# Two more weight buffers, x^T at two addresses and a longer entry into the feed-forward, in a two-layer retention and attention trunk

## The chip, the cores and the metric

The kernel runs on one core of a Trainium2 chip. The metric is the device time of one execution in microseconds (us).

## The reference

512 tokens of width 1024 pass through two layers. Layer 0 mixes tokens by retention, layer 1 by dilated attention; each mixer and each feed-forward is added to 1.41 x and normalised.

```python
def swiglu_ffn(x, w_up, w_down):
    gate, up = jnp.split(x @ w_up, 2, axis=-1)      # D_FF = 2816 each
    return (jax.nn.silu(gate) * up) @ w_down

for i in range(DEPTH):                              # DEPTH = 2
    mix = retention(x, ...) if i % 2 == 0 else dilated_attention(x, ...)
    x = _layer_norm(DEEPNORM_ALPHA * x + mix, ln_gain[i, 0], ln_bias[i, 0])
    x = _layer_norm(DEEPNORM_ALPHA * x + swiglu_ffn(x, w_up[i], w_down[i]), ...)
```

## The kernel before

**Products.** Every large operand is split into a high and a low float32r part, and each product is three matmuls (`mm3`): high by high, high by low, low by high. The activations are kept transposed (`xhi`, `xlo`, called x^T here) and in rows (`r0` to `r3`, four blocks of 128 tokens).

**Weights.** `Weights` streams blocks of 128x1024 f32 (512 KB) in the order of a plan that is written down ahead. A load (SP queue, L77) takes one of six buffers `wraw`; load n needs the buffer of load n-6 to have been used up. ACT copies a block to `whi` (L133) and DVE subtracts to get `wlo` (L134); four pairs of them exist.

**Feed-forward.** The up-projection is done by Strassen-Winograd: the gate and the up half of 256 columns each form a *quad*, which takes seven *parts* instead of eight: B11, B21, T2, T1, T3, B22, T4. A part is 24 matmuls of 128x256 (8 positions times 3). The x side of a part is a combination of quarters of x^T made once (`x_sums`, `x_more`; the names of parts are the names of these tiles, B11, B21, B22 and T1 lie in x^T itself). The weight side is, for parts T2, T3 and B22, a sum of blocks that DVE makes for each quad (`make_sum`, L107: `sum2`, `sum4`, `sum5`). A quad loads four blocks, n to n+3. `sum2` is block n minus block n+2, into which block n+3 has been added by a second, accumulating transfer from HBM (`add_blocks`, issued by POOL, L89), which can only start once n+2 has landed. After a part, ACT copies the bank (`copied`, L739) since the next part goes on adding in it: T3 may only start when `u2`, the copy after T2, is made. DVE adds B11's copy and B21 (L752), and ACT takes the SiLU (L753).

There are 11 quads per feed-forward, in chunks of 4, 4 and 3, and after each chunk the down-projection `rows_product` adds to `r`. `make_sum` for a quad is called when the part before it is split, so the sums of the next quad stand in DVE's order among the work of this one. A scheduler then sets each engine's order.

**Entry.** The last `rows_product` of a mixer finishes one row block after the other: add (L454), layer norm (`ln`, L344 to L353), eight transposes (`flush`, then `to_xt`, L387), ACT's copies with gain and bias (L403), splits (L275, L276). The first chunk therefore begins with `up_pending`: B11 and B21 of two quads need only the early blocks; `up_late` then does quad 0 in the order B22, T1, T2, T4, T3. In attention's last `rows_product` the last pair's quotients (`att_norm`, L1120, L1121) come in four parts of 128 tokens.

**Addresses.** Worked out from the sizes of the pools, x^T, the T tiles, the feed-forward's h, retention's z, q, k, v and s all begin 32 bytes past a multiple of 128 in each partition; `whi` and `wlo` begin 96 past.

Of the kernel before, what the change touches and what calls it, by code (L numbers as in the profile page):

```python
# [37 lines left out]
S0 = 7 * P  # L38

# [109 lines left out]
def trunk(tc, a, out):  # L149
# [41 lines left out]
    with tc.tile_pool(name="const", bufs=1) as cpool, tc.tile_pool(  # L191
        name="xpool", bufs=1
    ) as xpool, tc.tile_pool(name="wraw", bufs=6) as wraw, tc.tile_pool(
        name="pad", bufs=1
    ) as pad, tc.tile_pool(name="whl", bufs=4) as whl, tc.tile_pool(name="lnp", bufs=2) as lnp, tc.tile_pool(
        name="ps", bufs=8, space=PSUM
    ) as ps, tc.tile_pool(name="scratch", bufs=1, space=DRAM) as dr:
        pad.tile([P, 80], F32, name="pad")
        ws = Weights(nc, plan, wraw, whl, 2, 6)
# [48 lines left out]
class Core:  # L248
    def __init__(self, nc, tc, a, out, ws, cpool, xpool, lnp, ps, dr):
        self.nc, self.tc, self.a, self.out, self.ws = nc, tc, a, out, ws  # L250
        self.lnp, self.ps, self.dr = lnp, ps, dr
        self.xhi = xpool.tile([P, KT, T], F32R, name="xhi")
        self.xlo = xpool.tile([P, KT, T], F32R, name="xlo")
# [7 lines left out]
        nc.gpsimd.dma_start(out=self.cols, in_=a["ln_cols"])  # L261
        self.on_read = False
        self.pending = []
        self.halves = False

# [66 lines left out]
    def next_halves(self, i):  # L332


        self.halves, self.of = True, i

# [119 lines left out]
    def rows_product(self, zs, first, last, final=False, have=(), without=(), finish=False):  # L456
# [15 lines left out]
        w = [*have] + [self.ws.get() for _ in range(n - early - len(have))]  # L472
        for b in range(NB):
            if not early:
                banks.update({(b, h): self.bank() for h in range(2)})
# [13 lines left out]
            if last:  # L489
# [4 lines left out]
                if b == 2 and not final:  # L494
# [7 lines left out]
    def retention(self):  # L502
        nc, tc, a = self.nc, self.tc, self.a
        with tc.tile_pool(name="rt", bufs=1) as rt:
# [6 lines left out]
            nc.sync.dma_start(out=self.sin, in_=a["sin"])  # L511
            qk = self.ret_qk()
# [4 lines left out]
            self.next_halves(0)  # L517
            for h in range(RH):
# [12 lines left out]
                else:  # L531
# [6 lines left out]
                    z = self.ret_z(g, tr)  # L538
                    self.rows_product(z, False, True)
# [156 lines left out]
    def ffn(self, i):  # L696
        nc, tc = self.nc, self.tc
        with tc.tile_pool(name=f"ff{i}", bufs=1) as ff:
# [7 lines left out]
            self.x_late = {}  # L706
            for n in ("T2", "T3", "T4"):
                self.xs[n] = [ff.tile([P, 4, T // 2], F32R, name=f"{n}{p}") for p in ("hi", "lo")]
            for ch, n in enumerate(FC):
# [10 lines left out]
                self.halves = False  # L720
                self.rows_product(zs, ch == 0, last, final=last and i == 1, finish=ch == 0)
# [99 lines left out]
    def attention(self, first, steps):  # L821
        nc, tc = self.nc, self.tc
        with tc.tile_pool(name="at", bufs=1) as at:
# [6 lines left out]
            self.half = at.tile([P, HD], F32, name="half")  # L830
            nc.vector.memset(self.half, 1.0)
# [16 lines left out]
    def bias_rows(self):  # L848
# [6 lines left out]
        nc.gpsimd.dma_start(out=rb[0:32, :], in_=self.a["rbT"])  # L855
        nc.gpsimd.dma_start(out=oh0, in_=self.a["onehot"][:, 0:W0])
        nc.gpsimd.dma_start(out=oh1, in_=self.a["onehot"][:, W0:WB])
# [223 lines left out]
    def att_pv(self, p, _):  # L1081
# [25 lines left out]
        for h in range(2):  # L1107
            self.mm(den[h * HD : (h + 1) * HD], self.half, e[:, h], True, True)
        self.pv = bk, den, e

    def att_norm(self, p, _):
# [6 lines left out]
        for c in range(parts):  # L1118
# [3 lines left out]
            self.split(hi[:, c], lo[:, c], zf[:, c])  # L1122
        self.zs[p] = (hi, lo)

# [123 lines left out]
```

## Time and profile before

| | us |
|---|---|
| median of 3 runs (1700.6 to 1705.23) | 1703.7 |
| the profiled execution | 1714.11 |
| its span, from first to last instruction | 1712.3 |
| TensorE busy in it | 1654.3 |
| VectorE (DVE) busy | 1067.7 |
| ScalarE (ACT) busy | 648.4 |
| GpSimd (POOL) busy | 220.5 |

PE is the matmul engine. Its mean granted clock is 0.982 of full speed. A line such as L270 is that of `mm`, through which all products go, so groups of matmuls are told apart by their tiles.

### The profile page before, as it was taken

What the parts mean: (1) busy time and instruction counts of PE and PEld (TensorE: products, weight loads), DVE (VectorE), ACT (ScalarE), POOL (GpSimd) and SP (SyncE); (2) the same over time, 40 slices, a digit from 0 to 9 for tenths busy, and PEclk for the clock granted to TensorE, in tenths of its full rate; (3) what the DMA queues carried; (4) which work ended last, traced back from release to release, by engine and by line L of the source; (5) the groups of instructions that cost most, each with busy time, mean ns of one, the idle gap of its engine ahead of it and who ended that gap; (6) DMA issues with size and microseconds to landing.
All of it is one profiled execution on the core that took longest, in us unless ns stands there. A gap on an engine that the chain in (4) does not pass through costs nothing. (4 is left out here: it accounts for less than half of the span.)

```text
span 1712.3 us, 24333 instructions
## 1 busy us (share of the span) xinstructions
PE 1654.3 (97%) x9972; PEld 1432.7 (84%) x9972; DVE 1067.7 (62%) x1391; ACT 648.4 (38%) x937; POOL 220.5 (13%) x307
## 2 busy tenths in 40 slices
PE   9999999999899899899999999999999899989997
PEld 6888888888898898899878788788877898888896
DVE  6454454647994674657265574567569995575565
ACT  4322232325652451444332332333233752443351
POOL 0000000000000000006232332233311000000002
PEclk9999999999999999899999999999999999999999
DMA  7322223222453433433232223223321444334321
GB/s 276 129 71 96 74 72 101 87 74 79 126 166 106 115 114 94 114 111 100 98 95 79 86 87 87 87 76 97 88 74 50 117 130 148 99 112 134 90 84 50
DMA packets 52896, 174.33 MB, mean 102 GB/s; under 512 B 7764, under 2 KB 9828, under 8 KB 52784
## 3 DMA queue, kind: packets, MB, share of 16 engines
q1 hardware_dynamic: 44272, 155.81, 27.1%
q0 software_dynamic: 8512, 16.97, 5.6%
q8 instruction: 78, 1.28, 0.3%
q14 instruction: 34, 0.28, 0.1%
HBM read 170.57 MB, written 2.17 MB: 101 GB/s over the span
## 5 line engine op out<-in xcount | busy, mean ns | idle before, releaser
L134 DVE TENSOR_TENSOR wlo<-wraw,whi 128x1024 fp32r<-128x1024 f32 (+1 forms) x278 | 339.8, 1228 | 361.2 <-ACT whi L133 360.1
L133 ACT ACTIVATE whi<-wraw 128x1024 fp32r<-128x1024 f32 (+1 forms) x278 | 292.7, 1055 | 675.3 <-PE bank L270 357.7
L270 PE MATMUL bank<-xhi,whi 128*128 128x256 f32 (+1 forms) x1376 | 459.4, 334 | 9.1 <-ACT xhi L275 8.4
L270 PE MATMUL bank<-xhi,wlo 128*128 128x256 f32 (+1 forms) x1376 | 456.3, 332 | 3.6 <-DVE wlo L134 3.6
L270 PE MATMUL bank<-xlo,whi 128*128 128x256 f32 (+1 forms) x1376 | 455.8, 331 | 1.5 <-DVE xlo L276 1.5
L270 PEld LDWEIGHTS bank<-xhi,whi 128*128 128x128 f32 x1376 | 261.3, 190 | 40.2 <-ACT xhi L275 11.4
L270 PEld LDWEIGHTS bank<-xhi,wlo 128*128 128x128 f32 x1376 | 261.4, 190 | 32.5 <-DVE wlo L134 4.8
L270 PEld LDWEIGHTS bank<-xlo,whi 128*128 128x128 f32 x1376 | 261.6, 190 | 28.3 <-DVE xlo L276 2.1
L270 PE MATMUL bank<-whi,hlo 128*128 128x512 f32 x352 | 138.7, 394 | 0.0
L270 PE MATMUL bank<-wlo,hhi 128*128 128x512 f32 x352 | 138.0, 392 | 0.0
L270 PE MATMUL bank<-whi,hhi 128*128 128x512 f32 x352 | 136.8, 389 | 0.0
L882 POOL DMA_DIRECT2D tab<-rows_dram x128 | 69.5, 552 | 198.5 <-DVE s L1006 196.1
L133 ACT ACTIVATE whi<-sum 128x1024 fp32r<-128x1024 f32 x66 | 70.1, 1063 | 62.6 <-PE bank L270 51.9
L89 POOL DMA_DIRECT2D wraw<-in_w_up_dram x22 | 19.1, 869 | 559.3 <-DMA wraw<-in_w_up_dram 276.0
L454 DVE TENSOR_TENSOR r<-r,bank 128x512 f32<-128x512 f32 x78 | 52.3, 683 | 57.3 <-PE bank L270 57.3
L270 PE MATMUL bank<-whi,xlo 128*128 128x512 f32 (+1 forms) x256 | 86.0, 336 | 0.0
L270 PE MATMUL bank<-whi,xhi 128*128 128x512 f32 (+1 forms) x256 | 86.0, 336 | 0.0
L270 PE MATMUL bank<-wlo,xhi 128*128 128x512 f32 (+1 forms) x256 | 85.7, 335 | 0.0
L134 DVE TENSOR_TENSOR wlo<-sum,whi 128x1024 fp32r<-128x1024 f32 x66 | 80.4, 1220 | 8.1 <-ACT whi L133 8.1
L270 PE MATMUL bank<-T3hi,whi 128*128 128x256 f32 x176 | 57.8, 328 | 25.6 <-ACT tmp L739 25.6
L270 PEld LDWEIGHTS bank<-wlo,hhi 128*128 128x128 f32 x352 | 66.1, 188 | 15.1
L270 PEld LDWEIGHTS bank<-whi,hhi 128*128 128x128 f32 x352 | 66.1, 188 | 14.4
(279 smaller groups left out, 3006.2 us busy)
## 6 DMA issues: line engine op xcount, KB each, us to landing
wraw<-in_w_up_dram SPq DMA_DIRECT2D x88, 512.0 KB, 3.6
wraw<-in_w_aqk_dram SPq DMA_DIRECT2D x48, 512.0 KB, 3.5
wraw<-in_w_dn_dram SPq DMA_DIRECT2D x44, 512.0 KB, 3.6
wraw<-in_w_av_dram SPq DMA_DIRECT2D x24, 512.0 KB, 3.5
wraw<-in_w_up_dram POOLq DMA_DIRECT2D x22, 512.0 KB, 6.5
wraw<-in_w_rv_dram SPq DMA_DIRECT2D x16, 512.0 KB, 4.2
wraw<-in_w_rg_dram SPq DMA_DIRECT2D x16, 512.0 KB, 4.9
wraw<-in_w_ro_dram SPq DMA_DIRECT2D x16, 512.0 KB, 3.5
```

Source lines behind the costliest of these rows:

```text
L89: self.nc.gpsimd.dma_start(out=self.raw_tiles[u], in_=a[n + 3], accum_op=ALU.add)
L133: self.nc.scalar.activation(hi[:, c], src[:, c], AF.Copy)
L134: self.nc.vector.tensor_tensor(out=lo[:, c], in0=src[:, c], in1=hi[:, c].bitcast(F32), op=ALU.subtract)
L270: self.nc.tensor.matmul(out=out, lhsT=lhsT, rhs=rhs, start=start, stop=stop, skip_group_check=self.on_read)
L454: nc.vector.tensor_tensor(out=dst, in0=dst, in1=bk, op=ALU.add)
L882: self.nc.gpsimd.dma_start(out=tab[r * RUN : (r + 1) * RUN, h, b * P : (b + 1) * P].rearrange("p (r l) -> p r l", r=RES), in_=src(h * WB + ...
```

## The change

It has these parts:

1. `wraw` has eight buffers. Room comes from the removed `half` tile and pad, and from halving `dynamic_dma_scratch_size` (16384 by default, now 8192). The pools stand in another order.
2. x^T lies in a tile that is 128 floats longer, at offset 0 for retention and attention, and at offset 48 floats (192 bytes) while a feed-forward reads it (`place_x`). The T tiles get a pad of the same size ahead. By the sizes of the pools, everything now begins 96 bytes past a multiple of 128, weights too, except x^T in the feed-forward and the T tiles, which begin 32 past as before.
3. `up_pending` takes three quads instead of two: q0 B11, transposes, q0 B21, q1 B11, transposes, and so on. `up_late` still does quad 0.
4. The last pair's quotients are not issued together but one block at a time, inside `rows_product`.
5. In attention's last `rows_product`, transposes are called for after products (1,1) and (3,0) of block 3, not at block 2 and after (1,0).
6. The loads of `cols`, the bias rows' operands (`rbT`, `onehot`) and the first two `decay` tables go from POOL's queue to SP's.

```diff
-                todo.sort(key=lambda t: (t[1] if t[0] < 2 and t[1] < 2 else 2))
-                todo[4:9] = [(0, j) for j in (5, 3, 2, 6, 4)]
+                todo.sort(key=lambda t: t[0] >= EARLY or t[1] > 1)
+                todo[2 * EARLY : 2 * EARLY + 5] = [(0, j) for j in (5, 3, 2, 6, 4)]
...
-        ws = Weights(nc, plan, wraw, whl, 2, 6)
+        ws = Weights(nc, plan, wraw, whl, 2, 8)
...
-        self.xhi = xpool.tile([P, KT, T], F32R, name="xhi")
-        self.xlo = xpool.tile([P, KT, T], F32R, name="xlo")
+        self.xt = [xpool.tile([P, KT * T + P], F32R, name=n) for n in ("xhi", "xlo")]
+        self.place_x(0)
...
+    def place_x(self, shift):
+        self.xhi, self.xlo = [
+            t[:, shift : shift + KT * T].rearrange("p (k t) -> p k t", t=T) for t in self.xt
+        ]
...
         w = [*have] + [self.ws.get() for _ in range(n - early - len(have))]
+        at = ((1, 1), (3, 0)) if have else ((1, 0),)
         for b in range(NB):
+            while self.norm_parts and self.norm_parts[0][0] <= b + 1:
+                self.norm_parts.pop(0)[1]()
...
-                if last and not final and b == 3 and (i, h) == (1, 0):
+                if last and not final and b == 3 and (i, h) in at:
                     self.flush(1)
...
-                if b == 2 and not final:
+                if b == 2 and not final and not have:
                     self.flush(1)
...
-        nc.gpsimd.dma_start(out=dec, in_=self.a["decay"][h])
+        (nc.sync if h < 2 else nc.gpsimd).dma_start(out=dec, in_=self.a["decay"][h])
...
+            ff.tile([P, SHIFT], F32, name="pad")
             for n in ("T2", "T3", "T4"):
...
-                    quads = [self.up_late(*first[0]), self.up_rest(*first[1])]
+                    quads = [self.up_late(*first[0])]
+                    quads += [self.up_rest(*t) for t in first[1:]]
...
-        a = [self.up_first() for _ in range(2)]
-        self.flush(1)
-        a[0] = self.up_second(a[0])
-        self.flush()
-        a[1] = self.up_second(a[1])
-        return a
+        res = []
+        for _ in range(EARLY):
+            t = self.up_first()
+            self.flush(1)
+            res.append(self.up_second(t))
+        return res
...
-        nc.gpsimd.dma_start(out=rb[0:32, :], in_=self.a["rbT"])
+        nc.sync.dma_start(out=rb[0:32, :], in_=self.a["rbT"])
...
-    nc = bacc.Bacc("TRN2", target_bir_lowering=False, num_devices=1)
+    nc = bacc.Bacc("TRN2", target_bir_lowering=False, num_devices=1, dynamic_dma_scratch_size=8192)
```

**First place: DVE in the first quad of the second chunk.** The names are numbered here: before, blocks n, n+1, n+2 and n+3 of the next quad are `wraw_4375`, `wraw_4381`, `wraw_4393` and `wraw_4573`; now they are `wraw_4313`, `wraw_4345`, `wraw_4377` and `wraw_4384`. Before:

```order
L134 TENSOR_TENSOR wlo_4504<-sum2_4391,whi_4503 128x1024
L134 TENSOR_TENSOR wlo_4535<-wraw_4310,whi_4534 128x1024
L134 TENSOR_TENSOR wlo_4568<-sum4_4538,whi_4567 128x1024
L107 TENSOR_TENSOR sum2_4706<-wraw_4375,wraw_4393 128x1024
L752 TENSOR_TENSOR tmp_4564<-tmp_4531,bank_4533 128x512
L134 TENSOR_TENSOR wlo_4605<-sum5_4571,whi_4604 128x1024
```

Now (L109 is the old L107, L136 the old L134, L769 the old L752):

```order
L136 TENSOR_TENSOR wlo_4506<-sum2_4394,whi_4505 128x1024
L136 TENSOR_TENSOR wlo_4537<-wraw_4248,whi_4536 128x1024
L109 TENSOR_TENSOR sum2_4709<-wraw_4313,wraw_4377 128x1024
L136 TENSOR_TENSOR wlo_4570<-sum4_4540,whi_4569 128x1024
L109 TENSOR_TENSOR sum4_4776<-sum2_4709,wraw_4384 128x1024
L769 TENSOR_TENSOR tmp_4566<-tmp_4533,bank_4535 128x512
L136 TENSOR_TENSOR wlo_4608<-sum5_4573,whi_4607 128x1024
```

The next quad's `sum2` stands one row earlier, and its `sum4` now stands ahead of the addition that the SiLU waits for. In the later quads of a chunk `sum2` stands ahead of L809 (the old L792) instead of behind it.

**Second place: DVE at the first feed-forward's entry,** from the layer norm of the last row block on; `sum2`, `sum5` and `sum4` are quad 0's. Before:

```order
L350 BN_AGGR mv_3193<-st_3189 128x2
L134 TENSOR_TENSOR wlo_3248<-wraw_2935,whi_3247 128x1024
L323 TENSOR_SCALAR veps_3196<-mv_3193 128x1
L107 TENSOR_TENSOR sum2_3251<-wraw_2746,wraw_2987 128x1024
L353 TENSOR_SCALAR r3_86<-r3_86,mv_3193,rs_3194 128x1024
L107 TENSOR_TENSOR sum5_3253<-sum2_3251,wraw_2882 128x1024
L276 TENSOR_TENSOR xlo_80<-hlo_3289,xhi_79 128x4x128
L428 TENSOR_TENSOR hhi_3305<-hlo_3289,xw0_81 128x512
L107 TENSOR_TENSOR sum4_3445<-sum2_3251,wraw_2993 128x1024
L276 TENSOR_TENSOR xlo_80<-hhi_3305,xhi_79 128x4x128
L430 TENSOR_TENSOR hhi_3305<-hhi_3305,hlo_3289 128x512
L134 TENSOR_TENSOR wlo_3314<-sum5_3253,whi_3313 128x1024
```

Now:

```order
L359 BN_AGGR mv_3193<-st_3189 128x2
L109 TENSOR_TENSOR sum2_3372<-wraw_2567,wraw_2987 128x1024
L331 TENSOR_SCALAR veps_3196<-mv_3193 128x1
L348 TENSOR_TENSOR r0_79<-r0_79,gain_3204 128x1024
L362 TENSOR_SCALAR r3_82<-r3_82,mv_3193,rs_3194 128x1024
L284 TENSOR_TENSOR xlo_76<-hlo_3253,xhi_75 128x4x128
L437 TENSOR_TENSOR hhi_3269<-hlo_3253,xw0_77 128x512
L136 TENSOR_TENSOR wlo_3278<-wraw_2779,whi_3277 128x1024
L439 TENSOR_TENSOR hhi_3269<-hhi_3269,hlo_3253 128x512
L284 TENSOR_TENSOR xlo_76<-hhi_3269,xhi_75 128x4x128
L769 TENSOR_TENSOR tmp_3305<-tmp_3246,bank_3276 128x512
L284 TENSOR_TENSOR T2lo_3211<-hhi_3269,T2hi_3210 128x4x128
```

Quad 0's `sum5` comes eight rows further down, after the splits of two more early parts. On PE one part (B21 of quad 1, 24 matmuls) stood between the last transposes and quad 0's B22; now three stand there (B21 of quad 1, B11 and B21 of quad 2, 72 matmuls).

**Third place: SP's queue at the start,** from the second head's gate weights on (`rv`, `rg`, `rqk` are retention's weights). Before:

```order
L77 DMA wraw<-in_w_rg_dram 128x1024 x4
L77 DMA wraw<-in_w_rqk_dram 128x1024
L516 DMA r_85<-in_x_dram 128x1024
L516 DMA r_86<-in_x_dram 128x1024
L867 DMA rows_dram<-r_84 16x672
```

Now:

```order
L79 DMA wraw<-in_w_rg_dram 128x1024 x4
L79 DMA wraw<-in_w_rqk_dram 128x1024 x2
L870 DMA r_82<-in_rbT_dram 32x48
L871 DMA r_82<-in_onehot_dram 33x672
L872 DMA r_81<-in_onehot_dram 33x512
L79 DMA wraw<-in_w_rqk_dram 128x1024
L636 DMA dec<-in_decay_dram 128x512
```

The operands of the bias rows, which POOL issued in the first microseconds, now stand behind ten loads of weights.

## Rows read from the trace of the kernel before

**Rows 1.** Page, costliest groups: T3's high-by-high matmuls. After the bar: busy us, mean ns, idle before.

```profile
L270 PE MATMUL bank<-T3hi,whi 128*128 128x256 f32 x176 | 57.8, 328 | 25.6 <-ACT tmp L739 25.6
```

**Rows 2.** Timelines of SP, POOL, DVE, ACT and PE, 546 to 563: start, us, engine, instruction.

```profile
547.05 5.17 SPq L77 DMA_DIRECT2D wraw<-in_w_up_dram  x3
...
551.07 0.86 POOL L89 DMA_DIRECT2D wraw<-in_w_up_dram  x1 [33.38 <-DVE wlo L134]
...
557.93 1.23 DVE L107 TENSOR_TENSOR sum<-wraw 128x1024 f32<-128x1024 f32 x1 [4.15 <-DMA wraw<-in_w_up_dram]
...
559.79 0.63 ACT L753 ACTIVATE tmp<-tmp 128x512 f32<-128x512 f32 x1 [4.54 <-DVE tmp L752]
...
561.90 0.38 PE L270 MATMUL bank<-T3hi,whi 128*128 128x256 f32 x1 [2.20 <-ACT tmp L739]
```

**Rows 3.** Transfers issued between 546 and 563: KB each, us to landing.

```profile
wraw<-in_w_up_dram POOLq DMA_DIRECT2D x1, 512.0 KB, 6.8
```

**Rows 4.** Busy time by stretch: us; PE, PEld, DVE, ACT, POOL; granted clock; DMA share, GB/s.

```profile
548.63:638.18 89.55, 82.66 (x673) 81.86 (x672) 60.95 (x65) 44.41 (x58) 2.58 (x3) 0.94 0.42 123
682.13:750.06 67.93, 62.42 (x505) 61.83 (x504) 44.98 (x48) 33.06 (x43) 1.73 (x2) 0.92 0.40 123
1465.27:1556.53 91.26, 82.28 (x673) 81.49 (x672) 60.87 (x65) 44.40 (x58) 2.58 (x3) 0.94 0.41 121
1600.48:1668.82 68.34, 61.94 (x506) 61.35 (x504) 44.80 (x48) 33.07 (x43) 1.72 (x2) 0.93 0.36 107
619.14:638.18 19.04, 19.04 (x170) 19.04 (x169) 12.87 (x15) 11.46 (x15) 0.00 (x0) 1.00 0.34 111
561.90:566.37 4.47, 4.47 (x25) 4.47 (x26) 3.53 (x4) 1.38 (x2) 0.00 (x0) 0.62 0.18 44
```

**Rows 5.** The same view, the two entries, sixteen parts each.

```profile
417.45:472.04 54.59, 49.84 (x400) 48.05 (x401) 52.64 (x68) 38.30 (x64) 4.01 (x4) 0.97 0.50 135
1330.66:1388.68 58.02, 52.32 (x401) 51.11 (x401) 53.60 (x69) 39.10 (x65) 3.48 (x4) 0.91 0.48 130
```

**Rows 6.** Timelines of DVE and PE at the entries.

```profile
421.17 0.20 DVE L350 BATCH_NORM_AGGREGATE mv<-st 128x2 f32<-128x12 f32 x1
...
427.53 0.37 PE L270 MATMUL bank<-xhi,whi 128*128 128x256 f32 x1
...
1321.85 1.06 PE L387 MATMUL bank<-ident,r 128*128 128x128 f32 x8 [2.84 <-DVE r L353]
```

**Rows 7.** PE alone; 96, 24, 192, 168 matmuls: us; busy; clock; DMA share, GB/s.

```profile
57.37:79.82 22.45, 22.45 (x99) 1.00 0.31 105
81.21:86.65 5.44, 5.44 (x26) 1.00 0.28 96
638.18:682.13 43.95, 43.95 (x195) 1.00 0.29 87
472.04:491.08 19.04, 19.04 (x170) 1.00 0.40 139
```

**Rows 8.** Groups of PE by shape: busy us, mean ns, idle before.

```profile
L270 PE MATMUL bank<-xhi,whi 128*128 128x512 f32 x608 | 243.2, 401 | 1.6 <-ACT xhi L275 1.6
...
L270 PE MATMUL bank<-whi,hhi 128*128 128x512 f32 x352 | 136.8, 389 | 0.0
```

**Rows 9.** Timelines of SP and PE at the start.

```profile
26.04 0.45 SPq L77 DMA_DIRECT2D wraw<-in_w_rqk_dram  x1
...
29.41 1.30 PE L270 MATMUL bank<-r 33*16 33x336 f32 x4
```

**Rows 10.** Transfers issued between 26 and 34.

```profile
wraw<-in_w_rqk_dram SPq DMA_DIRECT2D x1, 512.0 KB, 5.2
```

**Rows 11.** Timelines of POOL and DVE, a pair's bias tables in attention.

```profile
872.81 8.69 POOL L882 DMA_DIRECT2D tab<-rows_dram  x16 [28.97 <-DVE s L1006]
...
903.30 0.68 DVE L985 TENSOR_TENSOR s<-bank,tab 128x512 f32<-128x512 f32 x1
```

**Rows 12.** Page, DMA issues: the bias tables.

```profile
tab<-rows_dram POOLq DMA_DIRECT2D x128, 16.0 KB, 2.0
```

More of the change, by code (lines that the diff above doesn't have):

```diff
@@ L38 @@
 S0 = 7 * P
+SHIFT = 48
+EARLY = 3
 class Weights:
@@ L191, in trunk @@
     with tc.tile_pool(name="const", bufs=1) as cpool, tc.tile_pool(
[L192 to L195, printed above, removed]
+        name="lnp", bufs=2
+    ) as lnp, tc.tile_pool(name="xpool", bufs=1) as xpool, tc.tile_pool(
+        name="wraw", bufs=8
+    ) as wraw, tc.tile_pool(name="whl", bufs=4) as whl, tc.tile_pool(
         name="ps", bufs=8, space=PSUM
     ) as ps, tc.tile_pool(name="scratch", bufs=1, space=DRAM) as dr:
-        pad.tile([P, 80], F32, name="pad")
-        ws = Weights(nc, plan, wraw, whl, 2, 6)
+        ws = Weights(nc, plan, wraw, whl, 2, 8)
         c = Core(nc, tc, a, out, ws, cpool, xpool, lnp, ps, dr)
@@ L260, in __init__ @@
         self.cols = cpool.tile([P, 2, 2, KT], F32, name="cols")
-        nc.gpsimd.dma_start(out=self.cols, in_=a["ln_cols"])
         self.on_read = False
@@ L264, in __init__ @@
         self.halves = False
+        self.norm_parts = []
+    def place_x(self, shift):
+        self.xhi, self.xlo = [
+            t[:, shift : shift + KT * T].rearrange("p (k t) -> p k t", t=T) for t in self.xt
+        ]
     def bank(self):
@@ L335, in next_halves @@
         self.halves, self.of = True, i
+        self.place_x(SHIFT)
     def finish(self, b):
@@ L511, in retention @@
             nc.sync.dma_start(out=self.sin, in_=a["sin"])
+            nc.sync.dma_start(out=self.cols, in_=a["ln_cols"])
             qk = self.ret_qk()
@@ L538, in retention @@
                     z = self.ret_z(g, tr)
+                    self.next_halves(0)
                     self.rows_product(z, False, True)
@@ L706, in ffn @@
             self.x_late = {}
+            ff.tile([P, SHIFT], F32, name="pad")
             for n in ("T2", "T3", "T4"):
                 self.xs[n] = [ff.tile([P, 4, T // 2], F32R, name=f"{n}{p}") for p in ("hi", "lo")]
+            ff.tile([P, P - SHIFT], F32, name="pad2")
             for ch, n in enumerate(FC):
@@ L720, in ffn @@
                 self.halves = False
+                self.place_x(0)
                 self.rows_product(zs, ch == 0, last, final=last and i == 1, finish=ch == 0)
@@ L829, in attention @@
             nc.vector.memset(self.ones.bitcast(F32), 1.0)
-            self.half = at.tile([P, HD], F32, name="half")
-            nc.vector.memset(self.half, 1.0)
             self.qt, self.kt = (
@@ L854, in bias_rows @@
         nc.gpsimd.memset(rb[32:33, :], NEG)
-        nc.gpsimd.dma_start(out=rb[0:32, :], in_=self.a["rbT"])
-        nc.gpsimd.dma_start(out=oh0, in_=self.a["onehot"][:, 0:W0])
-        nc.gpsimd.dma_start(out=oh1, in_=self.a["onehot"][:, W0:WB])
+        nc.sync.dma_start(out=rb[0:32, :], in_=self.a["rbT"])
+        nc.sync.dma_start(out=oh0, in_=self.a["onehot"][:, 0:W0])
+        nc.sync.dma_start(out=oh1, in_=self.a["onehot"][:, W0:WB])
         half = W0 // 2
@@ L1107, in att_pv @@
         for h in range(2):
-            self.mm(den[h * HD : (h + 1) * HD], self.half, e[:, h], True, True)
+            self.mm(den[h * HD : (h + 1) * HD], self.ones[:, 0:HD].bitcast(F32), e[:, h], True, True)
         self.pv = bk, den, e
@@ L1117, in att_norm, with part @@
         lo = at.tile([P, T], F32R, name="zlo", bufs=5)
-        for c in range(parts):
+        def part(c):
             c = slice(c * T // parts, (c + 1) * T // parts)
@@ L1123, in att_norm @@
         self.zs[p] = (hi, lo)
+        if parts > 1:
+            self.norm_parts = [(c, lambda c=c: part(c)) for c in range(parts)]
+        else:
+            part(0)
     def att_o(self, quad, _):
```

1 line of the change is left out of this document (removed).

## The prediction, made before the changed kernel was run

> **What bounds the kernel now.** PE is busy 1654.3 us of a span of 1712.3, so I looked for the time in which PE stands or runs slowly. In the page's costliest groups one row stands out: T3's first matmuls waited 25.6 us for ACT's copy L739, and take 328 ns in the mean [rows 1]. Next I read the stretches by quad. The last quad of a chunk takes 19.04 us for seven parts at a granted clock of 1.00, that is 2.72 us a part. The four stretches of the second and third chunks, 4, 3, 4 and 3 quads, take 89.55, 67.93, 91.26 and 68.34 us at a clock of 0.92 to 0.94 [rows 4]. The part after such a wait shows why: T3 takes 4.47 us with a granted clock of 0.62 in its stretch, against 2.72 [rows 4]. PE had stood for 2.20 us just before it [rows 2]. So a stall costs its wait and then a while of matmuls at the lower of PE's two clock levels, 1.2 instead of 2.4 GHz.
>
> The timelines name the chain [rows 2]. SP issued three loads from 547.05, when buffers came free. POOL could issue the accumulating transfer at 551.07, and it landed 6.8 us later [rows 3]. DVE waited 4.15 us for it, until 557.93, to make the `sum2` of the *next* quad. Behind that on DVE stands L752, which the SiLU waited for (4.54 us); on ACT the SiLU stands ahead of the copy L739, and that let T3 start at 561.90. The late thing is a weight buffer, 15 us upstream. DVE itself has room: 60.95 us busy of 89.55 in that stretch [rows 4].
>
> **The change, part by part.** All is reckoned against the profiled execution, 1714.1 us, which lies 10.4 above the median of 1703.7; the difference is taken off at the end.
>
> *Eight buffers.* Four clean quads are 76.16 us, three are 57.12. The four stretches exceed this by 13.39, 10.81, 15.10 and 11.22, together 50.5 us [rows 4]. A quad loads four blocks, so two more buffers move each load ahead by half a quad, some 9.5 us on a steady stream; the wait to be covered was 4.15 [rows 2]. Followed one by one: in a chunk's first quad, block n+2 no longer waits for the buffer freed at 547 but for one freed two loads earlier, while the down-projection still ran. The next quad's n+2 takes the last of the three slots from 547, so it is issued at about 552, lands with 4 us (547.05 to 551.07) at 556, and its accumulation lands 6.8 us later at 563; DVE reaches that `sum2` at about 567 when nothing waits (the quad ends at 548.63 + 19.04). In the third quad the slack is some 3 us by the same count. Against this, `sum2` now stands one row earlier and `sum4` stands ahead of the old L752 (the first of the order's excerpts): 1.2 us each less time. I take the whole 50.5. Bounds: 25 if every second stall stays, 50.5 if none does.
>
> *Three quads early, transposes, quotients.* Sixteen parts and 16 transposes take 16 x 2.72 + 1.6 = 45.1 us; the entries take 54.59 and 58.02 [rows 5], so 9.5 and 12.9 could be had behind B11. But DVE is busy 52.64 and 53.60 us of these [rows 5], and a different order of PE does not shorten its list. I followed DVE's new list with 1.14 us for a 128x1024 operation and 0.60 for a 128x512 (start to start). First entry: from 421.3, just after the row at 421.17 [rows 6], seven long operations, eleven short ones and a norm (0.73) come to 15.3, with 0.5 of waits for POOL: quad 0's B22 weights are ready at 437.1. PE, which takes up its parts at 427.53 [rows 6], is there after 72 matmuls (8.2 us) at 435.7 and waits 1.4. The same walk gives waits of 0.9 at quad 0's T3, 1.3 and 2.7 in quad 1, and the sixteenth part ends at 469.4 instead of 472.04: a gain of 2.6. Second entry: the wait of 2.84 for the first layer norm [rows 6] goes, since DVE reaches it 1.6 us earlier and PE 2.8 later. But block 3's quotient now stands behind two splits of weights and block 1's norm comes 1.2 later, so B11 gains 0.9 only. The walk then ends the sixteenth part at 1382.4 instead of 1388.68: 6.3, of which I give back 1.3 for a lower clock after the waits of 3 us that stay. Together 2.5 + 5 = 7.5; bounds 0 (DVE's list sets the end) and 15.
>
> *Addresses.* With the clock at 1.00, x-by-w matmuls of 512 columns follow each other at 22.45 / 96 = 233.9 ns, v-by-s at 5.44 / 24 = 226.7, w-by-h at 43.95 / 192 = 228.9 [rows 7]. By the addresses in the program, the first read one operand 32 and the other 96 bytes past a multiple of 128, the second both 32 past, the third 96 and 32. The changed kernel puts both at 96 for all three. If the like placement is what makes the second fast, 3 x 608 matmuls gain 7.2 ns and 3 x 352 gain 2.2 [rows 8]: 13.1 + 2.3 = 15.4 us. Against it speaks that parts of 256 columns, 32 against 96, run at 19.04 / 168 = 113.3 [rows 7], half of 226.7, so unlike places need not cost; the feed-forward keeps that placement. Between 0 and 15.4 (18 with the smaller groups) I take 15.4, since the three paces order themselves by placement. The Trainium skill (SBUF — State Buffer, section on the two separate sides) says the opposite: on the engine side only the port pair that DVE and GpSimd share causes contention, and PE's never waits for anyone. By that the sum would be 15.4 higher; it is the first rival.
>
> *Start.* The bias rows' matmuls run at 29.41 [rows 9]. Their operands now stand in SP's queue behind ten loads. The tenth should go out some 1 us before the ninth did (26.04, landing 5.2 later [rows 9, 10]), so the operands are issued around 25.5 and land around 31: 1.5 us of waiting, up to 4 with the lower clock, down to -0.5 because the first x^T competes with fewer transfers. I take +1.5.
>
> *At nothing:* the `ones` slice for `half`, the `decay` tables (used only after the first three products), the halved scratch (rival below).
>
> Sum: 1714.1 - 50.5 - 7.5 - 15.4 + 1.5 = 1642.2; less 10.4, **1632 us**.
>
> **The rivals.**
>
> *Placement does nothing.* PE's pace of 233.9 has another cause. Then 1632 + 15.4 = 1647. For it: the parts of 256 columns. Against it: the three paces above.
>
> *The accumulation is still late.* It lands 6.8 us after issue, and the slack in second and third quads is 3 to 4 us; transfers started earlier may run into others and take longer, and DVE's new order needs `sum4` as well. If half of the stalls stay, 1632 + 25 = 1657.
>
> *Slower than before: POOL's transfers run out of scratch.* The change halves what POOL's transfers have for their descriptions. The trace of before shows no wait for it: sixteen table transfers are issued in 8.69 us, 0.54 each [rows 11], while each lands 2.0 after its issue [rows 12], so some four are in flight. If with half the room each had to wait for the one before to land, sixteen would take 16 x 2.54 = 40.6 us, from 872.81 to 913.4, but DVE wants the table at 903.30 [rows 11]: 10.1 us late, in every second of eight pairs, 40 us. The accumulating transfers, far larger, would need two rounds of 6.8 and miss `sum2` again, which gives back the 50.5. That makes 1632 + 40 + 50 = 1722. It decides once a table issue takes over (903.30 - 872.81 - 2.0) / 16 = 1.8 us.
>
> **How the numbers follow.** Forecast 0.53, placement nothing 0.25, accumulation late 0.15 (half of it together with the former), scratch 0.04, more gained than reckoned (entries near their 15) 0.03. The forecast alone runs from 1620 to 1645. The range 1612 to 1662 leaves out the scratch case, the worse half of the late one and thin tails. A measurement of this kernel tells about 0.3%, 5 us, from no change. All cases but the scratch one and a chance of 0.01 to 0.02 beside it are faster by far more: faster 0.94, same 0.02, slower 0.04.
>
> **What would show it.** Right: no T3 row with idle time in the second and third chunks and each quad 19.0 us at clock 1.00; `sum2` without waits for the transfer; x-by-w at 227 ns; the sixteenth parts of the entries 2 to 7 us after B11's shorter than now; the bias-row matmuls waiting a microsecond or two. Wrong: DVE still waiting for `wraw` ahead of `sum2`, x-by-w at 233, POOL's issue of tables slower than 0.54, or a new wait in the entry larger than those removed.

## The result, and the profile after

| us | before | after |
|---|---|---|
| median | 1702.15 (4 runs, 1700.13 to 1705.23) | 1658.9 (4 runs, 1653.66 to 1659.6) |
| the profiled execution | 1714.11 | 1653.66 |
| its span | 1712.3 | 1651.5 |
| TensorE busy in it | 1654.3 | 1627.1 |
| mean granted clock | 0.982 | 0.997 |

The ratio is 0.9738, with an interval of 0.9711 to 0.9764. The forecast was 1632, in a range of 1612 to 1662: faster, and inside the range, but 27 us above the point. Note where the profiled executions lie: that of before 12 above the median in this table (10.4 above the 1703.7 that the prediction used), that of after 5 below its own.

PE's groups by shape in the profile of after. L278 is the old L270.

```profile
L278 PE MATMUL bank<-xhi,whi 128*128 128x512 f32 x608 | 240.7, 397 | 1.1 <-ACT xhi L283 1.1
...
L278 PE MATMUL bank<-T3hi,whi 128*128 128x256 f32 x176 | 49.3, 280 | 0.0
```

T3's 25.6 us of waiting [rows 1] are gone, and its mean fell from 328 to 280 ns. The waits of after (engine, line, releaser: us in total, times, longest) say why:

```profile
DVE sum L109 <- DMA wraw<-in_w_up_dram: 21.3, 4, 6.2
```

DVE still waits four times for a transferred block, but PE no longer waits for what comes behind it. All four waits end inside a down-projection, 9 to 14 us after its start; the longest is in the one from 1507.80 to 1551.32:

```profile
1517.66 1.22 DVE L109 TENSOR_TENSOR sum<-wraw 128x1024 f32<-128x1024 f32 x1 [6.21 <-DMA wraw<-in_w_up_dram]
```

Windows of after (columns as in [rows 4]): the two entries, sixteen parts each, then the first quads of the second and third chunks.

```profile
413.54:465.29 51.75, 48.55 (x400) 46.93 (x401) 51.31 (x65) 37.19 (x62) 3.96 (x4) 1.00 0.48 131
1298.90:1350.93 52.03, 49.83 (x401) 48.75 (x402) 50.84 (x64) 36.69 (x61) 4.01 (x5) 0.97 0.45 116
542.10:561.89 19.79, 19.79 (x170) 19.79 (x168) 16.23 (x17) 10.52 (x13) 0.85 (x1) 1.00 0.62 183
664.77:684.55 19.78, 19.78 (x169) 19.78 (x168) 16.22 (x17) 10.52 (x13) 0.85 (x1) 1.00 0.63 182
```

The entries are 2.84 and 5.99 us shorter than in [rows 5]. The quads show something new: PE is busy all the time, the clock is 1.00, and yet seven parts take 19.79 us, not the 19.04 of [rows 4]. A part takes 2.83 us instead of 2.72.

PE alone, columns as in [rows 7], as in all windows of PE below: 96 matmuls x-by-w, then 192 w-by-h, then four quads.

```profile
59.72:81.54 21.82, 21.82 (x98) 1.00 0.33 108
...
498.57:542.10 43.53, 43.53 (x194) 1.00 0.43 120
...
542.10:621.25 79.15, 79.15 (x674) 1.00 0.44 133
```

x-by-w now follows at 21.82 / 96 = 227.3 ns (233.9 in [rows 7]), and a down-projection takes 43.53 instead of 43.95. Retention, from its first v-by-s product to the feed-forward, fell from 337.63 us to 332.00, attention from 545.87 to 540.35.

PE at the start, and POOL's issue of a pair's tables:

```profile
30.82 1.29 PE L278 MATMUL bank<-r 33*16 33x336 f32 x4 [0.19 <-DMA r<-in_onehot_dram]
```

```profile
847.26 8.69 POOL L897 DMA_DIRECT2D tab<-rows_dram  x16 [28.40 <-DVE s L1021]
```

The bias rows' operands were just in time here (0.19 us). The tables go out in 8.69 us as in [rows 11], so half the scratch shows no wait.

By stages, span against span: start +1.7 (x0's first matmul to the first v-by-s, and its own beginning), retention -5.6, first entry up to the first down-projection -2.2, rest of that feed-forward -20.1, attention -5.5, second entry -4.4, rest of the second feed-forward -22.3, end -2.4 (behind the last matmul; no cause was looked for). Together -60.8.

### The profile page after: what moved, and what is told of

It reads as the page before. It is cut to its first block, busy times and chain, and to the rows that moved or that the text cites. A ratio compares the mean times of both kernels' runs of the same rounds, so it can differ in the third digit from the quotient of the medians.

```text
span 1651.5 us, 24315 instructions
## 1 busy us (share of the span) xinstructions
PE 1627.1 (99%) x9972; PEld 1423.9 (86%) x9972; DVE 1068.5 (65%) x1390; ACT 649.7 (39%) x937; POOL 216.2 (13%) x301
## 3 DMA queue, kind: packets, MB, share of 16 engines
q0 software_dynamic: 8192, 16.26, 5.7%
## 4 chain that ended last, share of the span: by engine, by line
PE 91%; DVE 6%; issue 1%; DMA 1%; ACT 1%; POOL 0%; DVEq 0%; SPq 0%; POOLq 0%; ACTq 0%
PE bank L278 90%; DVE wlo L136 2%; DVE sum L109 1%; DMA wraw<-in_w_up_dram 1%; PE bank L1042 0%; PE bank L688 0%; DVE xlo L284 0%; PE bank L396 0%; ACT xw L412 0%; DVE r L348 0%; DMA tmp<-in_xT_dram 0%; DVE r L463 0%; ACT whi L135 0%; DVE st L353 0%; DVE hlo L284 0%
## 5 line engine op out<-in xcount | busy, mean ns | idle before, releaser
L136 DVE TENSOR_TENSOR wlo<-wraw,whi 128x1024 fp32r<-128x1024 f32 (+1 forms) x278 | 340.1, 1227 | 356.1 <-ACT whi L135 354.5
L278 PE MATMUL bank<-xhi,whi 128*128 128x256 f32 (+1 forms) x1376 | 457.8, 333 | 6.2 <-ACT xhi L283 5.2
L278 PE MATMUL bank<-xhi,wlo 128*128 128x256 f32 (+1 forms) x1376 | 454.3, 330 | 1.9 <-DVE wlo L136 1.8
L278 PE MATMUL bank<-xlo,whi 128*128 128x256 f32 (+1 forms) x1376 | 454.0, 330 | 0.0
L278 PEld LDWEIGHTS bank<-xhi,whi 128*128 128x128 f32 x1376 | 259.7, 189 | 33.6 <-ACT xhi L283 7.4
L278 PEld LDWEIGHTS bank<-xhi,wlo 128*128 128x128 f32 x1376 | 262.2, 191 | 27.5 <-DVE wlo L136 3.1
L278 PEld LDWEIGHTS bank<-xlo,whi 128*128 128x128 f32 x1376 | 260.1, 189 | 23.1
L278 PE MATMUL bank<-whi,hhi 128*128 128x512 f32 x352 | 137.1, 390 | 0.0
L278 PE MATMUL bank<-wlo,hhi 128*128 128x512 f32 x352 | 137.0, 389 | 0.0
L278 PE MATMUL bank<-whi,hlo 128*128 128x512 f32 x352 | 137.0, 389 | 0.0
L278 PE MATMUL bank<-whi,xhi 128*128 128x512 f32 (+1 forms) x256 | 86.6, 338 | 0.9 <-DVE tmp L596 0.9
L278 PE MATMUL bank<-wlo,xhi 128*128 128x512 f32 (+1 forms) x256 | 86.1, 336 | 0.0
L278 PE MATMUL bank<-whi,xlo 128*128 128x512 f32 (+1 forms) x256 | 86.0, 336 | 0.0
L136 DVE TENSOR_TENSOR wlo<-sum,whi 128x1024 fp32r<-128x1024 f32 x66 | 80.3, 1219 | 5.7 <-ACT whi L135 5.6
L278 PEld LDWEIGHTS bank<-whi,hlo 128*128 128x128 f32 x352 | 66.1, 188 | 13.7
L278 PEld LDWEIGHTS bank<-wlo,hhi 128*128 128x128 f32 x352 | 66.1, 188 | 13.4
L278 PEld LDWEIGHTS bank<-whi,hhi 128*128 128x128 f32 x352 | 66.1, 188 | 13.4
```

What stands on the lines that cost most here:

```text
L136: self.nc.vector.tensor_tensor(out=lo[:, c], in0=src[:, c], in1=hi[:, c].bitcast(F32), op=ALU.subtract)
L278: self.nc.tensor.matmul(out=out, lhsT=lhsT, rhs=rhs, start=start, stop=stop, skip_group_check=self.on_read)
```

## The experiments

The first theory: the stalls hung on the number of buffers, and PE's pace hangs on where its two operands begin within 128 bytes. The rivals gave the gain to the places, the queues or the entries. As results came in, the questions became what sets a part at 2.72 or 2.83 us, and why the medians lie apart from the profiles. A distance below is the place of the x side less that of the weights, modulo 128 bytes: 64 in the feed-forward of before and after, 0 for the other products of after. Twelve kernels were run, each beside runs of before on its chip. Two kernels from different chips can be compared to about 3 us only: the medians of before lie between 1702.15 and 1705.38.

### Eight buffers alone

On the kernel before:

```diff
-    ) as xpool, tc.tile_pool(name="wraw", bufs=6) as wraw, tc.tile_pool(
+    ) as xpool, tc.tile_pool(name="wraw", bufs=8) as wraw, tc.tile_pool(
...
-        ws = Weights(nc, plan, wraw, whl, 2, 6)
+        ws = Weights(nc, plan, wraw, whl, 2, 8)
...
-            self.mm(den[h * HD : (h + 1) * HD], self.half, e[:, h], True, True)
+            self.mm(den[h * HD : (h + 1) * HD], self.ones[:, 0:HD].bitcast(F32), e[:, h], True, True)
...
-    nc = bacc.Bacc("TRN2", target_bir_lowering=False, num_devices=1)
+    nc = bacc.Bacc("TRN2", target_bir_lowering=False, num_devices=1, dynamic_dma_scratch_size=8192)
```

> The kernel before with eight weight buffers and nothing else of the change (the half tile and half of the scratch give the room; every address keeps its place modulo 128, entries, queues and orders are those of before). Theory A (the T3 stalls came from buffers alone; the slow pace of the 256-column parts in the changed kernel, 2.83 us a part instead of 2.72, is set by the 512-column products that run ahead of them at 226.7 ns): no T3 stall, parts in the second and third chunks at 2.72 us, quads 19.04, profiled execution near 1714 - 50 = 1664, ratio to before about 0.970. Theory B (a chunk without stalls settles at 2.83 us a part whatever the addresses, because only a stall puts the parts back to 2.72): quads 19.78, that is 10 us more, ratio about 0.976.

1660.84 us (before 1702.34); ratio 0.9752, 0.9737 to 0.9767. This one part gives 41.5 us, nearly what the whole change does. Windows of PE: the second feed-forward's first down-projection, a quad of the first feed-forward, and the quad behind that down-projection.

```profile
1396.16:1440.96 44.80, 44.80 (x194) 1.00 0.43 105
566.44:585.48 19.04, 19.04 (x171) 1.00 0.51 140
1440.96:1460.00 19.04, 19.04 (x169) 1.00 0.68 188
```

Quads run at 19.04 here, as theory A has it; that the ratio lies at theory B's 0.976 comes from A's 0.970 having been reckoned against the profiled execution of before. In the second feed-forward the parts had fallen to 2.83 in the first chunk, and were back at 2.72 after a down-projection that took 44.80 instead of 43.95, without PE having stood in between.

### Six buffers in the changed kernel

```diff
-        name="wraw", bufs=8
+        name="wraw", bufs=6
...
-        ws = Weights(nc, plan, wraw, whl, 2, 8)
+        ws = Weights(nc, plan, wraw, whl, 2, 6)
...
-EARLY = 3
+EARLY = 2
```

> The changed kernel with six weight buffers (and two quads early, since three need more than six; places, quotients, transposes and queues as changed). To be compared with the run with two quads early and eight buffers, 1663.7. Theory A (the buffers carry the gain, the rest of the change nearly cancels): the T3 stalls are back in the second and third chunks, 50 us, and a stall now and then puts the parts back to 2.72, so 42 to 50 us more than 1663.7: 1706 to 1714, that is no faster than the kernel before. Rival (the places and the entry carry a part of their own): 1685 to 1700.

1689.8 (before 1704.51); ratio 0.9921, 0.9904 to 0.9939: in the rival's band. Its waits:

```profile
DVE sum L109 <- DMA wraw<-in_w_up_dram: 60.1, 14, 6.4
...
PE bank L278 <- ACT tmp L756: 19.8, 12, 2.3
```

The stalls are back, twelve as before, though shorter (27.4 us in twelve before). Against the next kernel but one, which has eight buffers and two early quads, the two buffers are worth 26.1 here and 41.5 there. What the rest of the change brings without buffers is 14.7; on top of eight buffers it brings only about 2 (1660.84 against 1658.9).

The stalls do not always put the parts back to 2.72. In the second chunk of the second feed-forward a part starts after a wait of 2.31 us, and from there to the chunk's end the pace is 2.83; the last quad:

```profile
1487.30 0.39 PE L278 MATMUL bank<-T3hi,whi 128*128 128x256 f32 x1 [2.31 <-ACT tmp L756]
...
1518.31:1538.10 19.79, 19.79 (x170) 1.00 0.35 109
```

### x^T and T at the weights' place in the feed-forward

```diff
-SHIFT = 48
+SHIFT = 0
...
-            ff.tile([P, SHIFT], F32, name="pad")
```

> The changed kernel with x^T and the T tiles in the feed-forward at the same place modulo 128 as the weights (SHIFT = 0). Theory A: the shift matters to the parts; with like places the 256-column parts have their own pace, which may be 2.72 throughout (then about 11 us less than the changed kernel, some 1648) or slower than 2.83 (then more than 1659). Theory B (place does not matter to parts of 256 columns, the pace comes from what ran before): 2.83 us in the second and third chunks as in the changed kernel, time 1656 to 1661.

1665.55 (before 1702.34); ratio 0.9776, 0.976 to 0.9792. PE: a quad, and the down-projection ahead of it.

```profile
548.29:568.45 20.16, 20.16 (x170) 1.00 0.60 179
504.75:548.29 43.54, 43.54 (x194) 1.00 0.41 113
```

Every part takes 2.88 us. The like place that makes 512 columns fast (43.54) makes 256 columns slow: the reason for x^T's second place.

### Two early quads

```diff
-EARLY = 3
+EARLY = 2
```

> The changed kernel with the first two parts of two quads early instead of three (EARLY = 2; eight buffers, places and the other orders as changed). Theory A (three early quads gain as walked, 2.6 us at the first entry and part of the 6 at the second): 3 to 6 us slower than the changed kernel, 1662 to 1665. Rival (DVE's list sets the end of the entry in either order, and the gains at the entries come from the transposes and the quotients): within 1.5 us of the changed kernel.

1663.71 (before 1702.34); ratio 0.9769, 0.9754 to 0.9784. The median is 4.8 above that of after, within theory A's 3 to 6. From B11 to the first down-projection the entries take 88.68 and 91.24 us, against 85.03 and 86.23 with three.

### Old quotients and old transposes

```diff
-        at = ((1, 1), (3, 0)) if have else ((1, 0),)
+        at = ((1, 0),)
...
-                if b == 2 and not final and not have:
+                if b == 2 and not final:
...
-        if parts > 1:
-            self.norm_parts = [(c, lambda c=c: part(c)) for c in range(parts)]
-        else:
-            part(0)
+        for c in range(parts):
+            part(c)
```

> The changed kernel with parts 4 and 5 undone (all four quotients together, transposes at block 2 and after (1,0)); three quads early, eight buffers and the places as changed. Theory A (the walk: these two parts move B11 of the second feed-forward by about 1 us): 0 to 2 us slower. Theory B (they make most of the second entry's gain): 3 to 6 us slower.

1657.8 (before 1704.94); ratio 0.9713, 0.9688 to 0.9739, as after. Attention takes 540.36 (540.35), the second entry 85.30 (86.23): parts 4 and 5 are worth nothing that can be measured. How far an entry can be measured shows in the first one, which these two parts do not touch: 87.43 us here, 85.03 in after.

### h beside the T tiles, 64 from the weights

The down-projection's `hhi` and `hlo` move to distance 64 too.

```diff
-            ff.tile([P, 2, T], F32, name="hhi", bufs=FC[0])
+            ff.tile([P, SHIFT], F32, name="pad")
+            for n in ("hhi", "hlo"):
+                ff.tile([P, 2, T], F32R, name=n, bufs=FC[0])
...
-            ff.tile([P, SHIFT], F32, name="pad")
```

> The changed kernel with the feed-forward's h tiles at 32 past a multiple of 128, where the T tiles are, so that the down-projection reads unlike places again, as in the kernel before. Theory A: the down-projection goes back from 226.7 to 228.9 ns (+2.3 us), and the parts behind it run at 2.72 instead of 2.83 us (14 quads x 0.74 = -10.4): net -8, about 1651. Theory B (the pace of the parts has another cause): +2, about 1661, parts at 2.83.

1652.32 (before 1702.34); ratio 0.9706, 0.9688 to 0.9725. PE: a quad of the first feed-forward, the down-projection ahead of it, a quad of the second.

```profile
547.44:566.50 19.06, 19.06 (x169) 1.00 0.63 187
503.49:547.44 43.95, 43.95 (x194) 1.00 0.43 119
1367.15:1386.94 19.79, 19.79 (x171) 1.00 0.42 134
```

The down-projection is back at 43.95, and in the first feed-forward the parts behind it are back at 2.72. In the second they were at 2.83 ahead of it and stay there.

### h and T another 512 bytes on

As the last, with `SHIFT + P` floats of pad, to see whether the return to 2.72 in the first experiment comes from the place within a larger grid.

```diff
-            ff.tile([P, SHIFT], F32, name="pad")
+            ff.tile([P, SHIFT + P], F32, name="pad")
```

> The changed kernel with the h tiles and the T tiles of the feed-forward at 160 past a multiple of 1024 (704 past the weights modulo 1024, as in the kernel before), x^T in the feed-forward as changed. Theory A (the down-projection over unlike places sets the pace of the parts behind it, and with this distance it also brings slow parts back to 2.72, as in the run with eight buffers alone, where 192 matmuls took 44.80 us and the parts went from 2.83 to 2.72): all parts of the second and third chunks at 2.72, both feed-forwards near 255.5 from the first down-projection to the last, about 1649 to 1651. Theory B (that return was chance; the down-projection only keeps the pace that the entry left): as with h alone moved, 2.72 in one feed-forward and 2.83 in the other, or at random, 1652 to 1656.

1649.92 (before 1704.94); ratio 0.9671, 0.9646 to 0.9697. The second feed-forward's first down-projection and the quad behind it:

```profile
1386.62:1430.58 43.96, 43.96 (x194) 1.00 0.44 121
1430.58:1450.37 19.79, 19.79 (x170) 1.00 0.64 185
```

No return to 2.72 in this execution. In the profiles of the kernels with h moved, a down-projection at distance 64 keeps the pace that it meets; the return in the first experiment is the one exception. At distance 0 with x^T at 64 (after, and the kernels with six buffers, two early quads, old transposes or the loads back) it leaves 2.83 behind it every time.

The median lies in theory A's band all the same, and the profiled execution, 1656.35, is the slowest of its six. So it is with every kernel that moves h to 64: the profiled execution is the slowest, 4.3 to 6.4 above the median, while in the other kernels with eight buffers it lies 1.0 above it at most. Seven quads at 2.83 instead of 2.72 cost 5.2. The executions without a profile may therefore have run both feed-forwards at 2.72; no trace shows it.

### The small loads back on POOL's queue

Part 6 undone in the changed kernel, and then together with the last one:

```diff
+        nc.gpsimd.dma_start(out=self.cols, in_=a["ln_cols"])
...
-        (nc.sync if h < 2 else nc.gpsimd).dma_start(out=dec, in_=self.a["decay"][h])
+        nc.gpsimd.dma_start(out=dec, in_=self.a["decay"][h])
...
-        nc.sync.dma_start(out=oh0, in_=self.a["onehot"][:, 0:W0])
+        nc.gpsimd.dma_start(out=oh0, in_=self.a["onehot"][:, 0:W0])
```

> The changed kernel with part 6 undone: cols, rbT, onehot and the decay tables are issued by POOL again. Theory A (the start of the changed kernel is slower by the moved loads: from the first x-by-w matmul to the first v-by-s takes 75.1 us in its profile and 78.8 to 79.8 in those of its variants, 73.0 before): that stretch goes back to 73 less the gain in pace, and the kernel to about 1653 to 1655, 4 to 6 us faster than the changed one. Theory B (the start is slower because eight buffers let more weight loads in ahead; eight buffers alone showed 73.25, which speaks against it): within 2 us of the changed kernel.

> The changed kernel with both: loads back on POOL, h and T tiles at 160 past a multiple of 1024. Theory A of both: 9 to 13 us faster than the changed kernel, 1645 to 1650. If only one holds: 1650 to 1655. If neither: 1657 to 1662.

1651.33, ratio 0.9675 (0.9653 to 0.9698), 7.6 below after and, on the same chip, 6.5 below the kernel with old transposes; together **1643.89**, ratio 0.9633 (0.9609 to 0.9658), 6.0 below the kernel with h moved, on the same chip: the best version, ahead of both kernels (before 1704.94). Both lie 1 to 2 us below theory A's bands. SP and PE at the start, with the loads on SP (the kernel with h and T 512 bytes on), and what one load took from issue to landing:

```profile
22.22 0.42 SPq L871 DMA_DIRECT2D r<-in_rbT_dram  x1
...
r<-in_rbT_dram SPq DMA_DIRECT2D x1, 6.0 KB, 8.9
...
31.70 2.40 PE L278 MATMUL bank<-r 33*16 33x336 f32 x4 [3.36 <-DMA r<-in_onehot_dram]
...
36.33 0.63 PE L278 MATMUL bank<-wlo,xhi 128*128 128x512 f32 x1
```

With the loads on POOL, the same two of PE:

```profile
28.28 1.30 PE L279 MATMUL bank<-r 33*16 33x336 f32 x4
...
30.72 0.40 PE L279 MATMUL bank<-wlo,xhi 128*128 128x512 f32 x1
```

On SP the bias rows wait 3.36 us for their operands, and after this stand PE is granted its lower level: the same products take 0.63 us instead of 0.40. The next products begin at 35.73 instead of 30.38. The load of 6 KB was issued at 22.22, behind the weights, and took 8.9 us to land; POOL issued the same load at 2.57.

### The finish's gain and bias on POOL

On the best version:

```diff
-            self.nc.vector.tensor_tensor(out=self.r[b], in0=self.r[b], in1=t, op=op)
+            self.nc.gpsimd.tensor_tensor(out=self.r[b], in0=self.r[b], in1=t, op=op)
```

> The version with loads back on POOL and h and T at 160, and in it the products with gain and bias of the feed-forward's input rows (finish, 8 operations of 128x1024 per feed-forward) on POOL instead of DVE; nothing of the result changes. In the second feed-forward's first chunk the parts went from 2.72 to 2.83 at quad 2's B22, which waited 0.35 us for a wlo that stood behind such a product on DVE. Theory A (a short wait of that kind flips the pace of the parts, and the down-projection over unlike places then keeps it): with DVE relieved of 1.14 us twice ahead of that place the wait is gone, the parts stay at 2.72 and the second feed-forward takes 254.8 instead of 259.2 from its first down-projection to its last, total 1636 to 1640. Theory B (the flip has another cause, or POOL's work of 2.4 us each holds up the layer norms): 1642 to 1650 with parts at 2.83.

1672.09 (before 1704.51); ratio 0.9815, 0.9795 to 0.9836: 28 slower than the best. DVE and POOL at the first entry:

```profile
415.44 3.29 DVE L109 TENSOR_TENSOR sum<-wraw 128x1024 f32<-128x1024 f32 x1
418.65 0.14 DVE L332 TENSOR_SCALAR veps<-mv 128x1 f32<-128x1 f32 x1
418.76 3.30 DVE L109 TENSOR_TENSOR sum<-sum,wraw 128x1024 f32<-128x1024 f32 x1
424.81 2.82 DVE L363 TENSOR_SCALAR r<-r,mv,rs 128x1024 f32<-128x1024 f32 x1 [2.75 <-POOL rs L333]
```

```profile
411.94 5.70 POOL L349 TENSOR_TENSOR r<-r,gain 128x1024 f32<-128x1024 f32 x2 [8.11 <-ACT xhi L284]
417.60 6.67 POOL L349 TENSOR_TENSOR r<-r,bias 128x1024 f32<-128x1024 f32 x2
424.23 0.54 POOL L333 TENSOR_TENSOR rs<-veps,mhalf 128x1 f32<-128x1 f32 x1
```

The work that was to leave DVE slows what stays on it: `sum` takes 3.29 us beside POOL's products, 1.22 elsewhere. The last norm's `rs` also stands behind them on POOL. Each entry is 13 to 17 us longer (101.56 and 100.48 to the first down-projection, against 85.06 and 87.07), so both theories' times are missed. The paces changed places: a quad of the first feed-forward, then one of the second.

```profile
554.95:574.74 19.79, 19.79 (x170) 1.00 0.63 184
1456.90:1475.97 19.07, 19.07 (x170) 1.00 0.66 184
```

In the best version's profile the first is at 2.72 and the second at 2.83. Which feed-forward gets which pace is thus not given by the places.

### Two more distances, 32 and 96

On the best version, x^T (in the feed-forward), T and h begin 32 or 96 past the weights' place:

```diff
-SHIFT = 48
+SHIFT = 8
```

> The best version so far (1643.9), with x^T, the T tiles and the feed-forward's h placed 32 bytes further on in the 128-byte grid than the weights (they begin 0 past a multiple of 128, the weights 96) instead of 64. Theory C: the distance within 128 bytes decides; at 64 bytes parts of 256 columns have two paces (2.72 and 2.83 us), at 0 one slow pace (2.88), at 32 they have another set: either 2.72 always, then the second feed-forward loses its 2.83 and the time is 1637 to 1640, or a slower one, 2.83 to 2.88 throughout, then 1655 to 1665. Rival: any unlike place is the same; the first feed-forward at 2.72, the second at 2.83, 1641 to 1648. Down-projection: 43.95 us for 192 matmuls by the rival, something else by theory C.

1656.3 (before 1705.38); ratio 0.9713, 0.9695 to 0.9731. A quad and the down-projection ahead of it:

```profile
541.80:561.41 19.61, 19.61 (x169) 1.00 0.62 184
497.01:541.80 44.79, 44.79 (x194) 1.00 0.41 111
```

```diff
-SHIFT = 48
+SHIFT = 24
```

> The same with the three 96 bytes further on than the weights (they begin 64 past a multiple of 128, the weights 96). Theory C: as for a distance of 32, or the mirror of it; a pace that differs from 2.72 and 2.83 in one of the two feed-forwards, with 1637 to 1640 or 1655 to 1665. Rival: any unlike place is the same, 1641 to 1648, parts of the second feed-forward at 2.83, down-projection 43.95 us.

1667.26 (before 1705.38); ratio 0.9776, 0.9755 to 0.9796.

```profile
543.39:563.54 20.15, 20.15 (x169) 1.00 0.64 181
498.42:543.39 44.97, 44.97 (x195) 1.00 0.40 108
```

Each distance has paces of its own: theory C, on its slow side (1667.26 lies 2 above its band). All at clock 1.00 and with PE never idle:

| distance | part of 24 x 256 columns, us | 192 w-by-h of 512, us |
|---|---|---|
| 0 | 2.88 | 43.53 |
| 32 | 2.80, or 2.83 at the end of both first chunks | 44.79 |
| 64 | 2.72 or 2.83 | 43.95 (once 44.80) |
| 96 | 2.88 | 44.97 |

For 32 and 96 only the x side was moved, so there the table cannot tell the distance from the x side's own place. For 0 it can: 512 columns take 226.7 ns with both sides at 32 (v-by-s, [rows 7]) and with both at 96 (43.53 / 192). Nor do transfers explain the paces: a quad takes 19.04 at a DMA share of 0.68 (the first experiment) and 19.79 at 0.62 (after).

## Why the prediction was right, and where it was off

The direction and the main mechanism were right, and the time fell inside the range, but above the 1645 at which the forecast alone was to end. The 1658.9 stands next to the 1657 of the rival "the accumulation is still late", which the T3 row rules out. So it was the room left for rivals that kept the time inside the range; it held errors of another kind, nearly all on the slow side. Two of the prediction's signs also came out against it. The quads take 19.79 and not 19.0, and DVE still waits for `wraw` ahead of `sum2`; these waits lie where PE has a down-projection to do, and cost nothing.

**Eight buffers (-50.5): right in mechanism.** No T3 wait is left in the feed-forwards' later chunks, as said. The fourteen quads of after at 19.79 are 277.0 us, against 317.1 for the four stretches of [rows 4]: -40.1. At 19.04 they would be 266.6, the predicted -50.5. The stalls went; the difference of 10.4 is the pace, the next point.

**The step that failed: "parts of 256 columns, 32 against 96, run at 113.3, so unlike places need not cost; the feed-forward keeps that placement".** The placement of the parts was kept, the pace was not: fourteen quads at 2.83 instead of 2.72 a part took 10.4 us more. Before, the same places ran mostly at 2.72, straight behind a down-projection too; three parts there:

```profile
548.63:556.81 8.18, 8.18 (x73) 1.00 0.84 235
```

What the prediction left out is that the change puts the down-projection at distance 0, and that the parts behind such a one run at 2.83, whatever they ran at ahead of it. The first feed-forward of after shows it: the quad ahead takes 19.04, those behind 19.79, and moving h back to 64 gives it its 2.72. The quad ahead:

```profile
479.53:498.57 19.04, 19.04 (x171) 1.00 0.46 159
```

The second feed-forward was at 2.83 before its first down-projection. At distance 64 PE has two paces, and there the change falls on a wait of 0.35 us for `wlo`: three parts ahead of it take 8.16, three behind it 8.48.

```profile
1350.93:1359.09 8.16, 8.16 (x75) 1.00 0.63 184
1362.52:1371.00 8.48, 8.48 (x74) 1.00 0.48 175
```

That the wait chose the pace is not shown. A wait of the same length for the same thing in the first feed-forward left 2.72 behind it; the 214 matmuls that follow each of the two, first and second:

```profile
474.19:498.57 24.38, 24.38 (x215) 1.00 0.45 157
1359.83:1385.13 25.30, 25.30 (x214) 1.00 0.44 146
```

With six buffers waits of some 2 us left either pace behind them. What in PE holds the pace, what picks it, and why the return of the first experiment did not come again, stays open.

**Addresses (-15.4): right, 13.5.** Retention -5.6, attention -5.5, and the six down-projections together -2.3. The first rival, that placement does nothing, fell. But the move of h, part of the same change, also brought at least the first feed-forward's half of the 10.4 above. The Trainium skill (SBUF — State Buffer, section on the two separate sides) says that PE never waits for anyone on the engine side. The prediction took this to mean that places cost nothing; the table above, four distances at a clock of 1.00 with no idle time, shows that they do. Whether PE waits for another engine there, which is what the sentence denies, no run here shows.

**Entries (-7.5): right within what can be measured.** To the sixteenth part -2.84 and -5.99, where the walk gave 2.6 and 6.3; the 1.3 given back for the clock was not needed (0.97, against 0.91 before). To the first down-projection it is -2.2 and -4.4, since a wait of 0.35 us is left in each and the second's last parts run at 2.83. The first entry of after is the shortest of those with the same order of work and the same places of x^T (85.03 to 87.43 in six kernels), so the close agreement there is in part luck. The gain is the third quad's; quotients and transposes, which the walk weighed at under a microsecond net, give none.

**Start (+1.5): undersized.** The landing came where predicted (operands at 31.7, estimated 31), but by two errors that cancel: the loads were issued some 3 us earlier than the estimated 25.5 and took 8.9 us instead of 5.2. And the price of the stand was not the wait alone: 3.36 us, then products at the lower clock, 6.0 to 7.6 us by the kernels that undo it. The prediction's bound of 4 was too low. The profiled execution of after hit a start with a wait of only 0.19, so its stage shows +2.1 from the first matmul of x0; the five other kernels with eight buffers and the loads on SP waited 2.7 to 4.1 in theirs.

**The offset (-10.4): the second step that failed.** The forecast took the profiled execution's distance to the median off at the end, as if both kernels had it. But the execution of before seems to have been slow just where the change works. With eight buffers alone the profiled execution lies 0.4 above its median, so the offset goes with the stalls: by profiled executions that step is worth 52.9, by medians 41.5. So some 10 us were taken off twice, once in the stall term and once as offset. This is argued from medians, since no second execution of before was traced. On the other side the execution of after, with its lucky start, lies 5.2 below its median. The books close: 1653.66 is 11.5 above the 1642.2 of the sum (pace +10.4, addresses +1.9, entries +0.9, start +0.2, end -2.4, and 0.4 more outside the span), and 10.4 + 5.2 = 15.6 is the offset; together 27.1.

**The other rivals.** No accumulation was late enough to stop PE. The scratch is no limit (8.69 us for sixteen tables).

## What to carry to other kernels

A stall term read from one execution must be held against that execution's distance to the median before it is added to an offset: they can be the same microseconds. When a stall goes, look at what PE's pace is without it, matmul by matmul at full clock; operands' places within 128 bytes are worth some per cent either way, with the best place different for 256 and 512 columns, and each choice must be measured, with the products that run ahead of it. A small load that everything waits for belongs on a queue with nothing ahead of it: here a wait of PE of 3.36 us cost 6.0, the rest of it in clock.

## What the runs showed of the hardware that was not expected

- At a granted clock of 1.00 and with PE never idle, a matmul of 256 columns takes 113.3, 116.7, 117.8 or 120.0 ns (parts of 2.72, 2.80, 2.83, 2.88 us by 24), by the distance of its operands' places; at 64 and at 32 there are two paces at one distance, and each can last for hundreds of matmuls. For 512 columns 43.53 to 44.97 us by 192 are 226.7 to 234.2 ns.
- A wait of 3.36 us at the start is followed by products at 0.63 instead of 0.40 us; the stretch from 28.3 to 58.0 shows a granted clock of 0.83 there and 1.00 without the wait.
- DVE's operations of 128x1024 on two operands take 3.3 us beside POOL's products of the same kind, and 1.22 without. The Trainium skill (SBUF — State Buffer, section on the two separate sides) names the port pair that both share, with an exclusive lock; the rows agree: POOL's products took 2.3 to 3.4 us each, and DVE's took as long beside them.
